# Attention whose probabilities below the diagonal are turned by DMA, in an order timed for all engines

## The chip, the cores and the metric

The program runs on one core of one Trainium2 chip. The metric is the device time in microseconds (us) of one execution. Three runs of the kernel before took 3117.63, 3124.31 and 3127.85 us; the median is 3124.31. One more execution was profiled, and the views below are of that one. The engines are named as the profile names them: PE is TensorE (PEld its weight loads), DVE is VectorE, ACT is ScalarE, POOL is GpSimd, SP is SyncE, which issues DMAs.

## What is computed

The program is a trunk of two layers on 2048 rows of 1024 numbers: a Mamba-2 mixer, then latent attention with 16 heads, an output projection and a norm. The change is in the attention alone. Its heart in the reference:

```python
def causal_block_attention(q_nope, q_rope, k_nope, k_rope, v):
    ...
        s = jnp.einsum('bqhd,bkhd->bhqk', q_nope[:, q0:kv_len], k_nope[:, :kv_len]) + \
            jnp.einsum('bqhr,bkr->bhqk', q_rope[:, q0:kv_len], k_rope[:, :kv_len])
        s = s.astype(jnp.float32) * scale
        mask = (q0 + local)[:, None] >= jnp.arange(kv_len)[None, :]
        p = jax.nn.softmax(jnp.where(mask, s, -jnp.inf), axis=-1).astype(v.dtype)
        outs.append(jnp.einsum('bhqk,bkhd->bqhd', p, v[:, :kv_len]))
```

## The kernel before

Attention (`heads`, from L1214) works in jobs: head h of 16 by block qb of four blocks of 512 queries. A job has four row groups j of 128 queries. Each looks at the keys up to its own diagonal, cut into chunks of up to 512 (`cuts`). All operands are pairs of f16 numbers, a high and a low half, so that products come close to f32.

For a row group and chunk, TensorE makes the scores with three products (`mm3`, L86 to L88) in a PSUM bank, and adds the mask at the diagonal (L1257). VectorE takes the row maximum from PSUM (L1258), and over the chunks of a row group a small reduction (L1262). ScalarE takes the exponential (L1269) into a buffer `Pr` in SBUF, f32, and its sum.

The products with V need the probabilities the other way round, keys on the rows. So `turn` (L1277) makes, for 128 keys, up to four 128x128 f32 transposes on TensorE into a PSUM bank (L1282). ScalarE evicts the high half to f16 (L124), VectorE the low half (L125), into a buffer `PTs`. `values` (L1288) adds the two products with V (L1292, L1293). A finished job is evicted (L1299) and stored by two DMAs, one from SP (L1301), one accumulating from POOL (L1305). K, V and Q of the next head are loaded by DMAs from POOL (L1184, L1185, L1190, L1196 to L1198).

What sets the order: on TensorE the program's own order, in which the table CREDIT says after each score chunk how many turns (T) and products with V (V) follow, 20 chunks behind (LAG):

```python
        for credit in ahead():
            step += 1
            if step > LAG:
                for what in credit:
                    work(what)
```

The other engines' order is left to a scheduler that goes by priority. After attention `back` (L1350) loads its output again and multiplies it with the output weights, which ACT (L1368) and POOL (L1369) split.

Of the kernel before, what the change touches and what calls it, by code (L numbers as in the profile page):

```python
# [11 lines left out]
BF16 = mybir.dt.bfloat16  # L12
# [24 lines left out]
NP = 24  # L37
# [29 lines left out]
C1, C2, C3 = 6.28125, 1.93500518798828125e-3, 3.01991598196e-7  # L67


class Net:  # L70
# [374 lines left out]
    def constants(self, cp):  # L445
# [6 lines left out]
        self.mk = cp.tile([P, 2 * P], BF16, name="mk")  # L452
# [5 lines left out]
    def layer_constants(self, cp):  # L458
# [13 lines left out]
        nc.vector.memset(self.mk[:, P:], NEG)  # L472
# [24 lines left out]
        nc.vector.tensor_copy(self.mk[:, 0:P], self.mask)  # L497
# [681 lines left out]
    def load_k(self, h, lo, hi):  # L1179

        nc, ts = self.nc, slice(lo * TB, hi * TB)
        if lo == 0:
            self.keys[h] = self.t(self.hp, "K", [96, 2, T], F16, bufs=2)
        nc.gpsimd.dma_start(self.keys[h][0:64, :, ts], self.kn_d[h * 64:(h + 1) * 64, :, ts])  # L1184
        nc.gpsimd.dma_start(self.keys[h][64:96, :, ts], self.kr_d[:, :, ts])  # L1185

    def load_v(self, h):

        V = self.vals[h] = self.t(self.xq, "xT", [P, T // P, P], F16, bufs=8)
        self.nc.gpsimd.dma_start(V, self.v_d[:, h * P:(h + 1) * P].rearrange("(k p) d -> p k d", p=P))  # L1190

    def load_q(self, h, n):

        nc, ts = self.nc, slice(n * TB, (n + 1) * TB)
        Q = self.quer[h, n] = self.t(self.xq, "xT", [96, 2, TB], F16, bufs=8)
        nc.gpsimd.dma_start(Q[0:64], self.qn_d[h * 64:(h + 1) * 64, :, ts])  # L1196
        nc.gpsimd.dma_start(Q[64:80], self.q1_d[h * 16:(h + 1) * 16, :, ts])
        nc.gpsimd.dma_start(Q[80:96], self.q2_d[h * 16:(h + 1) * 16, :, ts])  # L1198
# [7 lines left out]
    def attention(self):  # L1206
        with ExitStack() as ctx:
# [3 lines left out]
            with self.tc.manual_schedule(engines={mybir.EngineType.PE}):  # L1211
                self.heads(sp)

    def heads(self, sp):  # L1214
        nc, v = self.nc, self.nc.vector
        begun = []
        keys, vals, quer = self.keys, self.vals, self.quer

        def cuts(kv):

            out, at = [], 0
            while at < kv:
# [323 lines left out]
```

## Time and profile before

| | us |
|---|---|
| median of three runs | 3124.31 |
| the profiled execution | 3126.91 |
| its span | 3125.1 |
| attention: first score product to last eviction | 2059.6 to 2938 |
| PE busy over the span | 3033.6 (97%) |
| DVE busy over the span | 2297.6 (74%) |
| ACT busy over the span | 1963.6 (63%) |
| POOL busy over the span | 609.5 (20%) |

In the views, a group's row reads: line, engine, operation, out<-in with partitions x elements, count, then busy us and mean ns of one, then the idle time ahead of it and what ended that. A duration is that of one record; records of one engine overlap a little, since an instruction begins while the one before drains. The window rows give busy time per engine in a stretch, with the count of instructions in brackets, the granted TensorE clock, the DMA share and GB/s. The chain of waits follows the work that ended last.

### The profile page before, as it was taken

The numbers are of one execution on the slowest core, as the hardware profiler recorded it, in microseconds if no ns is written. First come the engines' busy times: TensorE is split into PE (matmuls) and PEld (weight loads), VectorE is DVE, ScalarE is ACT, GpSimd is POOL, SyncE is SP. The second block draws the span as 40 slices with busy tenths as digits, with TensorE's granted clock in tenths as the row PEclk, the third lists the DMA queues.
The fourth block names the chain that finished last, engine by engine and source line by source line (L and its number), as shares of the span: only waits on it lengthen the run. The fifth ranks groups of instructions, "written<-read, shape, count | busy, mean of one in ns | idle before, by whom it ended". The sixth has DMA issues, their size and how long they took to land.

```text
span 3125.1 us, 50616 instructions
## 1 busy us (share of the span) xinstructions
PE 3033.6 (97%) x17815; PEld 1946.3 (62%) x17815; DVE 2297.6 (74%) x4548; ACT 1963.6 (63%) x4952; POOL 609.5 (20%) x855
## 2 busy tenths in 40 slices
PE   8999999999999999999999999999999999999998
PEld 6777754556556665556665455456666666666687
DVE  6878887788776687776755644468888888888676
ACT  7888576665656465654643433368888888888522
POOL 1222022111221112211111212222222222222100
PEclk9999999999999999999999999999999999999999
DMA  5343667655465454754457556632232323233485
GB/s 179 120 135 107 214 201 256 192 157 179 150 220 179 129 161 128 239 192 129 143 159 270 173 163 202 190 96 55 58 64 55 68 53 66 56 73 89 110 270 163
DMA packets 217138, 456.78 MB, mean 146 GB/s; under 512 B 29154, under 2 KB 71138, under 8 KB 215444
## 3 DMA queue, kind: packets, MB, share of 16 engines
q1 hardware_dynamic: 188980, 375.54, 38.2%
q0 software_dynamic: 27904, 78.02, 9.6%
q8 instruction: 140, 2.29, 0.3%
q14 instruction: 114, 0.93, 0.1%
HBM read 332.21 MB, written 121.25 MB: 145 GB/s over the span
## 4 chain that ended last, share of the span: by engine, by line
PE 52%; issue 10%; DVE 9%; ACT 8%; DMA 5%; POOL 3%; SPq 1%; POOLq 0%; ACTq 0%; DVEq 0%
PE mm L86 10%; PE mm L87 10%; PE mm L88 10%; PE tr L1282 7%; PE tr L1292 3%; PE tr L1293 3%; DVE cacc L691 2%; PE tr L86 1%; PE tr L88 1%; PE tr L87 1%; DMA wraw<-in_ssm_w_in_dram 1%; DMA big<-cumT 1%; PE tr L895 1%; ACT Pr L1269 1%; ACT Xw L888 1%
## 5 line engine op out<-in xcount | busy, mean ns | idle before, releaser
L125 DVE SCALAR_TENSOR_TENSOR PTs<-tr,PTs 128x512 f16<-128x512 f32 (+3 forms) x640 | 373.1, 605 | 96.2 <-ACT PTs L124 90.2
L1269 ACT ACTIVATE Pr<-mm,nm 128x512 f32<-128x512 f32 (+2 forms) x631 | 398.7, 642 | 15.0 <-DVE nm L1262 14.2
L124 ACT ACTIVATE PTs<-tr 128x512 f16<-128x512 f32 (+3 forms) x640 | 331.0, 545 | 115.8 <-PE tr L1282 106.8
L1258 DVE TENSOR_REDUCE mx<-mm 128x1 f32<-128x512 f32 (+2 forms) x569 | 336.1, 615 | 21.0 <-PE mm L88 17.7
L1282 PE MATMUL tr<-pack,Pr 128*128 128x128 f32 x2176 | 318.0, 273 | 2.2 <-ACT Os L1299 2.0
L86 PE MATMUL mm<-xT,wsp 128*128 128x512 f16 (+1 forms) x800 | 308.7, 386 | 0.3 <-ACT wsp L116 0.3
L87 PE MATMUL mm<-xT,wsp 128*128 128x512 f16 (+1 forms) x800 | 306.2, 383 | 0.0
L88 PE MATMUL mm<-xT,wsp 128*128 128x512 f16 (+1 forms) x800 | 304.9, 383 | 0.5 <-DVE wsp L117 0.5
L1282 PEld LDWEIGHTS tr<-pack,Pr 128*128 128x128 f32 x2176 | 253.6, 141 | 69.7 <-ACT Os L1299 2.8
L86 PE MATMUL mm<-wsp,xT 128*128 128x512 f16 (+2 forms) x640 | 233.9, 367 | 6.3 <-ACT craw L685 5.1
L691 DVE SCALAR_TENSOR_TENSOR cacc<-craw,pack,cacc 128x512 f32<-128x512 f32 x288 | 217.1, 773 | 28.4 <-ACT cacc L689 26.6
L87 PE MATMUL mm<-wsp,xT 128*128 128x512 f16 (+2 forms) x640 | 233.4, 365 | 1.4 <-DVE wsp L125 1.3
L88 PE MATMUL mm<-wsp,xT 128*128 128x512 f16 (+2 forms) x640 | 233.0, 365 | 0.0
L86 PE MATMUL mm<-K,xT 96*128 96x512 f16 (+2 forms) x639 | 224.0, 350 | 8.2 <-ACT Pr L1269 6.7
L88 PE MATMUL mm<-K,xT 96*128 96x512 f16 (+2 forms) x639 | 223.0, 349 | 0.0
L87 PE MATMUL mm<-K,xT 96*128 96x512 f16 (+2 forms) x639 | 222.4, 348 | 0.0
L1292 PE MATMUL tr<-PTs,xT 128*128 128x512 f16 (+3 forms) x640 | 221.4, 347 | 0.1
L1293 PE MATMUL tr<-PTs,xT 128*128 128x512 f16 (+3 forms) x640 | 219.5, 347 | 0.0
L86 PE MATMUL mm<-wsp,yT 128*128 128x512 f32 x512 | 210.4, 412 | 1.9 <-DVE sz L721 1.3
L87 PEld LDWEIGHTS <-xT 128*128 128x128 f16 (+1 forms) x1280 | 125.5, 98 | 130.8 <-issue 34.8
L844 POOL TENSOR_TENSOR Xp<-Xw,Xp 128x512 fp32r<-128x512 f32 x64 | 86.6, 1353 | 609.1 <-ACT Xp L843 579.2
L87 PE MATMUL mm<-wsp,yT 128*128 128x512 f32 x512 | 204.2, 399 | 0.0
(457 smaller groups left out, 6965.1 us busy)
## 6 DMA issues: line engine op xcount, KB each, us to landing
wsp<-wo_d SPq DMA_DIRECT2D x96, 512.0 KB, 4.0
wsp<-w_d SPq DMA_DIRECT2D x68, 512.0 KB, 4.4
wraw<-in_ssm_w_in_dram SPq DMA_DIRECT2D x128, 256.0 KB, 3.1
big<-cumT SPq DMA_DIRECT2D x64, 512.0 KB, 4.9
wo_d<-wsp SPq DMA_DIRECT2D x32, 512.0 KB, 3.4
w_d<-wsp SPq DMA_DIRECT2D x32, 512.0 KB, 3.4
st<-w_d SPq DMA_DIRECT2D x56, 256.0 KB, 3.0
wsp<-wu_d SPq DMA_DIRECT2D x28, 512.0 KB, 3.8
```

The costliest lines, as they stand in the source:

```text
L86: mm(out, l_hi, r_hi, start=start, stop=False)
L87: mm(out, l_hi, r_lo, start=False, stop=False)
L88: mm(out, l_lo, r_hi, start=False, stop=stop)
L124: self.nc.scalar.activation(hi, src, AF.Copy, scale=scale)
L125: self.nc.vector.scalar_tensor_tensor(lo, src, scale, hi, ALU.mult, ALU.subtract)
L691: nc.vector.scalar_tensor_tensor(acc, raw[:, k:k + TB], wk[k], acc, ALU.mult, ALU.add)
L844: nc.gpsimd.tensor_tensor(u[:, 1], x, u[:, 0].bitcast(F32), ALU.subtract)
L1258: v.tensor_reduce(mx[:, n:n + 1], s[:, :w], AX.X, ALU.max, negate=nb == 1)
L1269: nc.scalar.activation(x[:, :w], s[:, :w], AF.Exp, bias=nm, accum_out=sums[h][:, at, n:n + 1])
L1282: nc.tensor.transpose(pt[:, j * P:(j + 1) * P], st["P"][j][kb], self.ident)
L1292: nc.tensor.matmul(st["O"][:, c], vals[h][:, kb, :], u[:, 0], start=kb == 0, stop=False)
L1293: nc.tensor.matmul(st["O"][:, c], vals[h][:, kb, :], u[:, 1], start=False, stop=kb == nk - 1)
```

## The change

Attention's order is now written out for all five engines before anything is issued. A class `Pace` plays the jobs through with a fixed duration for each step and a number of buffers, and records the order in which the steps begin; `heads` then issues them in that order, and the scheduler leaves all engines as they are. The steps: S scores, M maximum, N shift, E exponential; T turn on TensorE, A and B the evictions of its high and low half; V products with V; F, O eviction and store; R, Y, Z the row sums.

Of the six chunks of 512 keys below the diagonal that a head has (one in block 1, two in block 2, three in block 3), five take another way (TURNED): H copies the 128x512 f32 of `Pr` to f16 on VectorE, L subtracts it from `Pr` on GpSimd for the low half, both in one buffer `HL`, and X is one DMA from SP that transposes the 128x1024 of both halves into a tile `PX`. Four such DMAs (one per row group) fill a `PX`, from which V reads directly. The four diagonal chunks and one more stay on TensorE. There are six `HL`, three `PX` and 18 `Pr` buffers (24 before).

Besides: the diagonal chunks have their exact width of 128 to 512 (before, 256 at least); the factor 2^15 moves from the evictions into the exponential's shift (PSHIFT), which makes N one or two small operations on each of 256 row groups; a score may be in any of eight PSUM banks; the loads of K, V and Q are issued from SP in place of POOL.

```diff
-NP = 24
-LAG = 20
-DEPTH = 2
-CREDIT = (
-    (("VT",), ("TV",), ("VT",), ("TV",)),
-    (("", "VTVT"), ("", "TTVV"), ("", "TTVV"), ("", "TTVV")),
-    (("TT", "", "VVTV"), ("TV", "", "VTTV"), ("TV", "", "TTVV"), ("TTV", "", "TVV")),
-    (("T", "", "", "VVTTVTV"), ("T", "V", "", "VTTVTV"), ("T", "V", "V", "TVTTV"), ("TV", "V", "", "TVTVT")),
-)
+ENGINES = ("PE", "ACT", "DVE", "POOL", "SP")
+BUFS = dict(ps=8, Pr=18, PTs=5, HL=6, PX=3)
+SCORED = 5
+DMA_DELAY = 4000
+TURNED = ((), (0,), (0, 1), (0, 1))
+def DVE(n):
+    return 62 + n * 1.042, 135
+PSHIFT = 10.397207708399179
...
+class Pace:
...
+    def __init__(self, turned):
+        self.turned, self.now, self.count = turned, 0.0, 0
+        self.jobs = [(h, qb) for h in range(NH) for qb in range(NB)]
...
+    def run(self):
+        while True:
+            for e, waiting in self.ready.items():
+                if self.until[e] <= self.now:
+                    fit = sorted((w for w in waiting if w[2]()), key=lambda w: w[:2])
+                    if fit:
+                        waiting.remove(fit[0])
+                        fit[0][3]()
+            if self.until["PE"] <= self.now:
+                self.tensor()
+            if not self.coming:
+                break
+            self.now = self.coming[0][0]
+            while self.coming and self.coming[0][0] <= self.now:
+                heapq.heappop(self.coming)[2]()
+        assert not (self.todo_s or self.todo_t or self.todo_v)
+        return self.order
...
+    def tensor(self):
+        f = self.free
+        if self.sums and f["ps"] > 0:
+            return self.rows(self.sums.pop())
+        if self.todo_s and f["ps"] > 0 and self.scored < SCORED:
+            return self.scores(*self.todo_s.pop())
+        if self.todo_t and f["ps"] > 0 and f["PTs"] > 0:
+            n, k = self.todo_t[-1]
+            if all((n, j, k // 4) in self.probs for j in range(self.first(n, k), 4)):
+                return self.turn(*self.todo_t.pop())
+        if self.todo_v and self.todo_v[-1] in self.pairs:
+            if self.todo_v[-1][0] in self.opened or f["ps"] > 0:
+                return self.values(*self.todo_v.pop())
...
+    def high(self, n, j, c):
+        self.give(HL=-1, PX=-((n, c) not in self.dma))
+        self.dma.setdefault((n, c), 4)
+        def low():
+            self.issue("POOL", ("L", n, j, c), 1364, 60, moved)
+        def moved():
+            self.give(Pr=1)
+            self.queue("SP", 1, lambda: self.issue("SP", ("X", n, j, c), 1300, DMA_DELAY, landed))
+        def landed():
+            self.give(HL=1)
+            self.dma[n, c] -= 1
+            if not self.dma[n, c]:
+                for k in range(4 * c, 4 * c + 4):
+                    self.pairs[n, k] = "PX"
+        self.issue("DVE", ("H", n, j, c), 345, 130, lambda: self.queue("POOL", 1, low))
...
-            with self.tc.manual_schedule(engines={mybir.EngineType.PE}):
+            with self.tc.manual_schedule():
...
+    def load_q(self, h, n, q=None):
+        q, ts = q or self.nc.gpsimd, slice(n * TB, (n + 1) * TB)
         Q = self.quer[h, n] = self.t(self.xq, "xT", [96, 2, TB], F16, bufs=8)
-        nc.gpsimd.dma_start(Q[0:64], self.qn_d[h * 64:(h + 1) * 64, :, ts])
-        nc.gpsimd.dma_start(Q[64:80], self.q1_d[h * 16:(h + 1) * 16, :, ts])
...
-                def exp(n, at=4 * qb + j, parts=parts, banks=banks, nm=nm, p=p):
-                    s, w = banks[n]
-                    x = self.t(sp, "Pr", [P, TB], bufs=NP)
-                    nc.scalar.activation(x[:, :w], s[:, :w], AF.Exp, bias=nm, accum_out=sums[h][:, at, n:n + 1])
-                    for c in range(0, w, P):
-                        p[(parts[n][0] + c) // P] = x[:, c:c + P]
...
-        def turn(h, qb, kb, st):
-            jj = max(kb - 4 * qb, 0)
-            pt = self.t(self.pp, "tr", [P, TB], bufs=4)
-            for j in range(jj, 4):
-                nc.tensor.transpose(pt[:, j * P:(j + 1) * P], st["P"][j][kb], self.ident)
-            c = slice(jj * P, TB)
-            u = self.t(sp, "PTs", [P, 2, TB], F16, bufs=5)
-            self.pair16(u[:, 0, c], u[:, 1, c], pt[:, c], PSCALE)
-            return u[:, :, c], c
...
+        def S(n, j, c):
+            h, qb = jobs[n]
+            if j == c == 0:
                 if qb == 0:
                     sums[h] = self.t(sp, "sum", [P, 16, 4], bufs=3)
                     nc.gpsimd.memset(sums[h], 0.0)
...
+                if h + 1 < NH:
+                    if qb == 2:
+                        self.load_k(h + 1, 0, NB, nc.sync)
+                        self.load_v(h + 1, nc.sync)
+                    self.load_q(h + 1, qb, nc.sync)
+            Q, K, w = quer[h, qb], keys[h], pace.width(n, j, c)
+            s, tag = bank("mm")
+            qs, ks = slice(j * P, (j + 1) * P), slice(c * TB, c * TB + w)
+            self.mm3(s[:, :w], Q[:, 0, qs], Q[:, 1, qs], K[:, 0, ks], K[:, 1, ks], True, c < qb)
+            if c == qb:
+                nc.tensor.matmul(s[:, w - P:w], self.idb, self.mk, start=False, stop=True)
+            if c == 0:
+                shifts[n, j] = self.t(sp, "nm", [P, 1], bufs=4)
+                maxima[n, j] = self.t(sp, "mx", [P, 4], bufs=4)
+            banks[n, j, c] = s, tag, w
+        def M(n, j, c):
+            s, _, w = banks[n, j, c]
+            v.tensor_reduce(maxima[n, j][:, c:c + 1], s[:, :w], AX.X, ALU.max, negate=True)
+        def N(n, j):
+            qb, m, nm = jobs[n][1], maxima.pop((n, j)), shifts[n, j]
+            if qb == 1:
+                v.tensor_scalar(nm, m[:, 0:1], m[:, 1:2], PSHIFT, ALU.min, ALU.add)
+                return
+            if qb:
+                v.tensor_reduce(nm, m[:, :qb + 1], AX.X, ALU.min)
+            v.tensor_scalar(nm, nm if qb else m[:, 0:1], PSHIFT, None, ALU.add)
+        def E(n, j, c):
+            h, qb = jobs[n]
+            s, tag, w = banks.pop((n, j, c))
+            x = probs[n, j, c] = self.t(sp, "Pr", [P, TB], bufs=BUFS["Pr"])
+            nc.scalar.activation(x[:, :w], s[:, :w], AF.Exp, bias=shifts[n, j],
+                                 accum_out=sums[h][:, 4 * qb + j, c:c + 1])
+            used[tag] -= 1
+        def H(n, j, c):
+            u = halves[n, j, c] = self.t(sp, "HL", [P, 2, TB], F16, bufs=BUFS["HL"])
+            v.tensor_copy(u[:, 0], probs[n, j, c])
+        def L(n, j, c):
+            u = halves[n, j, c]
+            nc.gpsimd.tensor_tensor(u[:, 1], probs.pop((n, j, c)), u[:, 0], ALU.subtract)
+        def X(n, j, c):
+            if (n, c) not in moved:
+                moved[n, c] = self.t(sp, "PX", [P, 8, TB], F16, bufs=BUFS["PX"])
+            u = halves.pop((n, j, c)).rearrange("p s c -> p (s c)")
+            nc.sync.dma_start(moved[n, c][:, :, j * P:(j + 1) * P], u, transpose=True)
+        def T(n, k):
+            jj = pace.first(n, k)
+            pt, tag = bank("tr")
+            for j in range(jj, 4):
+                nc.tensor.transpose(pt[:, j * P:(j + 1) * P],
+                                    probs[n, j, k // 4][:, k % 4 * P:(k % 4 + 1) * P], self.ident)
+            turned[n, k] = pt, tag, slice(jj * P, TB)
+        def A(n, k):
+            pt, tag, c = turned[n, k]
+            u = self.t(sp, "PTs", [P, 2, TB], F16, bufs=BUFS["PTs"])
+            nc.scalar.activation(u[:, 0, c], pt[:, c], AF.Copy)
+            turned[n, k] = pt, tag, c, u
+        def B(n, k):
+            pt, tag, c, u = turned[n, k]
+            v.tensor_tensor(u[:, 1, c], pt[:, c], u[:, 0, c], ALU.subtract)
+            turned[n, k] = u[:, 0, c], u[:, 1, c]
+            used[tag] -= 1
+        def V(n, k):
+            h, qb = jobs[n]
+            if n not in outs:
+                outs[n] = *bank("tr"), 4 * qb + 4
+            o, tag, left = outs[n]
+            if (n, k) in turned:
+                hi, lo = turned.pop((n, k))
+            else:
+                hi, lo = (moved[n, k // 4][:, s * 4 + k % 4] for s in range(2))
+            c = slice(pace.first(n, k) * P, TB)
+            nc.tensor.matmul(o[:, c], vals[h][:, k, :], hi, start=left == 4 * qb + 4, stop=False)
+            nc.tensor.matmul(o[:, c], vals[h][:, k, :], lo, start=False, stop=left == 1)
+            outs[n] = o, tag, left - 1
...
+        def O(n):
+            h, qb = jobs[n]
+            o = outs.pop(n)
+            od = self.o_d[h * 64:(h + 1) * 64, qb * TB:(qb + 1) * TB]
+            nc.sync.dma_start(od, o[0:64, :])
+            nc.gpsimd.dma_start(od, o[64:128, :], accum_op=ALU.add)
+            if h == NH - 3:
+                self.load_wo(qb)
+        steps = dict(S=S, M=M, N=N, E=E, H=H, L=L, X=X, T=T, A=A, B=B, V=V, F=F, O=O, R=R, Y=Y, Z=Z)
+        for what, *where in pace.run():
+            steps[what](*where)
```

How the instructions move. On TensorE, in the third head, before: four turns (`pack` holds the identity) stand between the products with V for one block of keys and the next.

```order
L1282 MATMUL tr_23273<-pack,Pr_22957 128x128
L1282 MATMUL tr_23273<-pack,Pr_23023 128x128
L1282 MATMUL tr_23273<-pack,Pr_23100 128x128
L1282 MATMUL tr_23273<-pack,Pr_23170 128x128
L1292 LDWEIGHTS xT_21890
L1292 MATMUL tr_23076<-PTs_23230,xT_21890 128x128
```

At such a place now, again TensorE in the third head: after the last diagonal block, the products read a `PX` with no turn ahead of them.

```order
L1508 MATMUL tr_23289<-PTs_23382,xT_21859 128x128
L1507 LDWEIGHTS xT_21859
L1507 MATMUL tr_23289<-PX_23079,xT_21859 128x512
L1508 LDWEIGHTS xT_21859
L1508 MATMUL tr_23289<-PX_23079,xT_21859 128x512
```

Moved: 16 turns per such chunk are gone from TensorE's order, and V now waits for a DMA there. On VectorE before, in the third head: maxima (`mx`), shifts (`nm`) and evictions (`PTs`) alternate.

```order
L1258 TENSOR_REDUCE mx_22956<-mm_22989 128x1
L1262 TENSOR_REDUCE nm_22955<-mx_22956 128x1
L125 SCALAR_TENSOR_TENSOR PTs_23000<-tr_22997,PTs_23000 128x256
L125 SCALAR_TENSOR_TENSOR PTs_23005<-tr_23003,PTs_23005 128x128
L125 SCALAR_TENSOR_TENSOR PTs_23015<-tr_23010,PTs_23015 128x512
```

VectorE now, in the fourth head (CAST is step H, L1493 step B):

```order
L1465 CAST HL_23308<-Pr_23179 128x512
L1465 CAST HL_23316<-Pr_23230 128x512
L1444 TENSOR_REDUCE mx_23302<-mm_23297 128x1
L1465 CAST HL_23329<-Pr_23252 128x512
L1444 TENSOR_REDUCE mx_23302<-mm_23323 128x1
L1493 TENSOR_TENSOR PTs_23327<-tr_23312,PTs_23327 128x384
L1444 TENSOR_REDUCE mx_23302<-mm_23333 128x1
L1465 CAST HL_23361<-Pr_23287 128x512
L1493 TENSOR_TENSOR PTs_23356<-tr_23341,PTs_23356 128x256
L1452 TENSOR_REDUCE nm_23301<-mx_23302 128x1
L1453 TENSOR_SCALAR nm_23301<-nm_23301 128x1
```

Moved: the evictions of the five chunks are gone; the casts stand in ones and twos between maxima, and 124 of the later 319 directly behind another cast. POOL before only issues DMAs and clears the sums (`xT` is a Q or V tile); its order now, for the casts just shown, is that of their subtractions.

```order
L1190 DMA xT_21890<-v_d 128x16x128
L1324 MEMSET sum_23178 128x64
L1305 DMA o_d<-Os_21755 64x512
L1196 DMA xT_21892<-qn_d 64x2x512
L1197 DMA xT_21892<-q_d 16x2x512
```

```order
L1540 DMA o_d<-Os_23293 64x512
L1469 TENSOR_TENSOR HL_23308<-Pr_23179,HL_23308 128x512
L1469 TENSOR_TENSOR HL_23316<-Pr_23230,HL_23316 128x512
L1469 TENSOR_TENSOR HL_23329<-Pr_23252,HL_23329 128x512
L1469 TENSOR_TENSOR HL_23361<-Pr_23287,HL_23361 128x512
```

Moved: the loads went to SP, where they stand between the transposing DMAs, and a subtraction follows each cast on POOL.

More of the change, by code (lines that the diff above doesn't have):

```diff
@@ L1317, in heads, with bank @@
-        jobs = [(h, qb) for h in range(NH) for qb in range(NB)]
-        states = [{"P": []} for _ in jobs]
-        sums = {}
-        def ahead():
-            for n, (h, qb) in enumerate(jobs):
+        pace = Pace(TURNED)
+        jobs = pace.jobs
+        used = {"mm": 0, "tr": 0}
+        sums, shifts, maxima, banks, probs, turned, halves, moved, outs = ({} for _ in range(9))
+        def bank(first):
+            tag = first if used[first] < 4 else "tr" if first == "mm" else "mm"
+            used[tag] += 1
+            return self.t(self.pp, tag, [P, TB], bufs=4), tag
```

244 lines of the change are left out of this document (139 added, 105 removed).

## The prediction

> **What bounds the kernel now.** I read the busy times by window first, because the edit touches one stage only. Attention runs from the first turned chunk at 2074 us to the last eviction at 2938 us:
>
> ```profile
> core 0: us, PE busy (x) PEld busy (x) DVE busy (x) ACT busy (x) POOL busy (x), PEclk, DMA share, GB/s
> 2074.00:2938.00 864.00, 854.76 (x5584) 563.68 (x5582) 734.38 (x1500) 716.60 (x1975) 196.48 (x294) 1.00 0.28 61
> 2938.00:2950.00 12.00, 9.62 (x42) 7.33 (x41) 2.14 (x3) 1.11 (x3) 0.82 (x1) 0.98 0.80 197
> ```
>
> TensorE is busy for 854.8 of 864 us at full granted clock, so in this stage it is the bound and it loses only 9 us. VectorE (734, 85%) and ScalarE (717, 83%) have about 15% of room, and GpSimd (196) stands almost idle. Busy time of TensorE is not the same as work at its peak, so I then read the groups of this window and the chain of waits:
>
> ```profile
> L125 DVE SCALAR_TENSOR_TENSOR PTs<-tr,PTs 128x512 f16<-128x512 f32 (+3 forms) x640 | 373.1, 605 | 96.2 <-ACT PTs L124 90.2
> L1282 PE MATMUL tr<-pack,Pr 128*128 128x128 f32 x2175 | 317.8, 273 | 2.2 <-ACT Os L1299 2.0
> ```
>
> ```profile
> 2930.75 0.44 PE tr L1282 x4
> 2937.74 0.60 ACT Os L1299
> 2949.07 0.50 PE mm L86
> ```
>
> The record of one turn (273 ns) overlaps its neighbours. In the chain four turns take 0.44 us, so one costs the path 0.109 us, and 2176 of them cost 237 us of the 864. Almost nothing waits in front of them (2.2 us). VectorE idles for ScalarE's PTs (90 us), so it is a follower now.
>
> **What is taken off TensorE.** Per head, ten chunks of probabilities exist: four diagonal, six below. Five of the six leave TensorE: 5 x 16 = 80 turns per head, 1280 of 2176. That is 1280 x 0.109 = 139.5 us. The first row block of each head is now 128 wide, not 256: three products and a mask of 128 fewer columns, 4 x 0.053 us x 16 heads = 3.4 us (a quarter of the 512-column step of 0.216 us between 2911.69 and 2911.91 below). The products with V stay the same in number and width. TensorE's own need becomes 854.8 - 139.5 - 3.4 = 712 us.
>
> ```profile
> 2911.69 0.38 PE L1292 MATMUL tr<-PTs,xT 128*128 128x512 f16 x1
> 2911.91 0.38 PE L1293 MATMUL tr<-PTs,xT 128*128 128x512 f16 x1
> ```
>
> **What it does to ScalarE and VectorE.** A chunk that is turned by DMA needs no PSUM evictions. 80 pairs of 128x512 become 20 per head; 320 of each of these two evictions go:
>
> ```profile
> 2300.82 1.28 DVE L125 SCALAR_TENSOR_TENSOR PTs<-tr,PTs 128x512 f16<-128x512 f32 x2
> 2301.80 0.61 ACT L124 ACTIVATE PTs<-tr 128x512 f16<-128x512 f32 x1
> 2302.28 0.71 ACT L1269 ACTIVATE Pr<-mm,nm 128x512 f32<-128x512 f32 x1
> ```
>
> Two on VectorE take 1.28 us with one tail of about 0.08, so 0.60 each; on ScalarE the next instruction starts 0.48 after the eviction. ScalarE falls to 717 - 320 x 0.48 = 563 us and cannot bind. VectorE loses 320 x 0.60 = 192 us and gains 320 casts of 128x512 f32 to f16 in SBUF (step H). No such cast is in the trace; the nearest is a one-source SBUF operation of the same size, and the nearest in GpSimd's new work is its f32 add/subtract:
>
> ```profile
> L1001 DVE TENSOR_SCALAR yt<-sz x4: 427/428/617, 1587.6 to 1863.8; 128x512 f32<-128x512 f32 x4
> L1262 DVE TENSOR_REDUCE nm<-mx x192: 135/156/158, 2064.2 to 2918.3; 128x1 f32<-128x2 f32 x64, 128x1 f32<-128x3 f32 x64, 128x1 f32<-128x4 f32 x64
> L844 POOL TENSOR_TENSOR Xp<-Xw,Xp x64: 1255/1288/2115, 89.7 to 1571.7; 128x512 fp32r<-128x512 f32 x64
> ```
>
> I take 0.428 less the same tail, 0.345 us: 320 x 0.345 = 110 us (ends: 0.345, or 0.60 if it runs like the eviction, +82 us). The shifts change from 192 small reductions to 128 reductions and 256 one-column operations, 192 more at 0.16 = 31 us. VectorE's own need: 734 - 192 + 110 + 31 = 683 us, below TensorE's 712. Without anything else the stage would be TensorE's.
>
> **The price that decides: VectorE and GpSimd share something.** GpSimd gains 320 subtractions (step L) of 1.29 us, 413 us, and gives up issuing the loads of K, V and Q. Here is what its operations do to VectorE's in the Mamba stage:
>
> ```profile
> 239.21 1.65 POOL L844 TENSOR_TENSOR Xp<-Xw,Xp 128x512 fp32r<-128x512 f32 x1
> 239.62 1.79 DVE L902 TENSOR_TENSOR y<-y,yt 128x512 f32<-128x512 f32 x1
> ```
>
> ```profile
> L902 DVE TENSOR_TENSOR y<-y,yt x60: 678/692/1796, 105.2 to 1573.3; 128x512 f32<-128x512 f32 x60
> L896 DVE TENSOR_TENSOR y<-y,tr x64: 670/686/690, 87.3 to 1571.6; 128x512 f32<-128x512 f32 x64
> L211 DVE TENSOR_SCALAR rr<-ri x4: 156/654/1216, 351.1 to 1414.2; 1x2 int32<-1x2 int32 x4
> ```
>
> L902 has both operands in SBUF. Alone it takes 0.69; started 0.41 us into GpSimd's Xp it took 1.79, and it ended 0.55 after that did, as if it could begin only when GpSimd was about done. L896 has one operand in PSUM and never exceeds 0.690. A one-source SBUF operation (L211, L1001) shows the same jump, 0.156 to 1.216 and 0.427 to 0.617. So maxima and evictions, which read PSUM, are safe beside L, and H is not: it reads and writes SBUF with one source. H runs beside L by design, since each L starts when its H ends and the next H follows soon.
>
> The Trainium skill, SBUF — State Buffer, section Who interferes with whom, states just this: a copy in a two-port mode and a GpSimd operation exclude one another for a whole instruction, while an operation with one SBUF input outside these modes doesn't contend. The rows above agree; it speaks against this change.
>
> The size: with a stage of about 800 us, L runs for 413/800 = 52% of it. An H that comes at any moment then waits 0.52 x 1.29/2 = 0.33 us; 320 of them, 107 us. Ends: 0 (each H slips in just before its L) and 320 x 1.29 = 413. I take 107, because the order has both kinds: 124 of the 319 later H stand directly behind another H and can start before the first one's L, the others have reductions and evictions between and meet a running L. The 256 one-column operations could wait in the same way, 256 x 0.33 = 86 us; I take 0, since one element per row gives a second port nothing to do where L211 has two, and keep 86 in the range.
>
> Behind a waiting H, VectorE's queue holds maxima and evictions: the next exponentials wait for the maxima, PSUM banks come free late, and TensorE starves. So these microseconds land on the path as soon as VectorE's sum passes TensorE's: 683 + 107 = 790 against 712. GpSimd itself stands at 196 less its 210 issues plus L:
>
> ```profile
> L1196 POOL DMA_DIRECT2D xT<-qn_d x56 | 34.5, 617 | 247.5 <-PE tr L1312 180.4 <-PE mm L1257 66.9
> L1198 POOL DMA_DIRECT2D xT<-q_d x56 | 32.2, 575 | 0.0
> L1197 POOL DMA_DIRECT2D xT<-q_d x56 | 29.2, 521 | 0.0
> L1190 POOL DMA_DIRECT2D xT<-v_d x14 | 17.0, 1212 | 55.0 <-PE mm L1257 55.0
> L1184 POOL DMA_DIRECT2D K<-kn_d x14 | 7.5, 537 | 0.0
> L1185 POOL DMA_DIRECT2D K<-kr_d x14 | 7.1, 507 | 0.0
> ```
>
> 196 - 127 + 413 = 482 us, and it waits for H in turn; at most 110 more. It does not bind.
>
> **The transposing DMAs (step X).** 320 of 128 x 1024 f16, 256 KB each, all from SP's queue, 84 MB in all. The trace has no transposing DMA. The nearest rows are a plain load of the same size, a load in 256-byte pieces, and what it costs a queue to issue one:
>
> ```profile
> st<-w_d SPq DMA_DIRECT2D x56, 256.0 KB, 3.0
> xT<-v_d POOLq DMA_DIRECT2D x16, 512.0 KB, 6.1
> L1301 SPq DMA_DIRECT2D o_d<-Os x64: 445/446/514, 2082.4 to 2938.4; - x64
> ```
>
> Issue: between 0.45 (one piece per row) and 1.21 (L1190, sixteen); at 1.2, 384 us, with 289 other issues at 0.45 it is 514 us of SP, hidden. Landing: 3 us if transposing costs nothing extra, 6 us if small pieces cost twice. Six H/L buffers hold a chunk for about 0.4 + 1.3 + 1.2 + 6 = 9 us, so six in 9 us, 1.5 us per chunk and 480 us in all: hidden in 804. I take 0. At what rate it stops being hidden is rival D. The Trainium skill, DMA: Bandwidth & Descriptors, section Latency and other measured facts, gives 261 GB/s for a transposing DMA with a strided middle dimension, by which one would take an estimated 1.0 us and all 322 us; that would be hidden too, and no run here shows it yet. The moved loads on SP stand behind X's that wait for GpSimd; they are issued about a head early, 804/16 = 50 us, which covers them.
>
> **Sum.** VectorE 790, plus the 9 us that the bounding engine lost before, plus about 5 at the end: the last chunk now goes L 1.3, X and landing 3 to 4 before its products. 804 against 864, 60 us less. The eviction-to-output gap of 11 us after 2938 (quoted in the chain) stays. The profiled execution took 3126.9 us (span 3125.1 and 1.8 around it): 3067. The median of the runs is 2.6 lower than that execution, so 3065.
>
> **Rivals.**
> - B, TensorE stays the bound. H mostly finds GpSimd between two L, which needs waits below (712 - 683)/320 = 0.09 us each. 712 + 9 + 5 = 726, 138 us less: 2987. For it: 124 H stand directly behind another one, and VectorE has slack before it binds (683 against 712). Against: L fills half the stage, so most other H must meet one.
> - C, the wait eats it all, slower. The place is VectorE at H. The waits reach 864 - 14 - 683 = 167 us when an H waits 0.52 us instead of 0.33; from there on the kernel is slower. If each of the 195 H that don't stand directly behind another one waits a whole L: 195 x 1.29 = 252, stage 949, 85 us more: 3210. For it: L902's 1.79, a nearly whole wait, and each L starts just behind its H; the order was made with engines that don't hinder each other. Against: then all engines wait, and gaps grow.
> - D, the transposing DMAs become the bound: one at a time at 2.66 us or more per chunk (850/320). At the 3.0 us of the plain load with no overlap, 960 + 14, 110 more: 3237. For it: nothing here shows two of them in flight. Against: the DMA share is 0.28 in this stage. The Trainium skill, VectorE: DVE Perf Modes, section The three transpose paths, lists 1309 ns for one 128x128 block by DMA; eight to a chunk one after another would be 10 us by estimate, far beyond that point.
> - E, VectorE lands about where TensorE was (790 with about 60 of the small operations' 86): within 9 us of before.
>
> **Numbers.** Forecast 0.48, B 0.20, C 0.14, D 0.10, E 0.08. Below 0.3% (9 us) this measurement can't tell from no change. Faster: B and nearly all of the forecast, 0.66; same: E and the forecast's upper edge, 0.10; slower: C and D, 0.24. The forecast's own range is 3000 to 3120 (waits of 0.12 to 0.5 us per H). The full range is 2982, just under B, to 3180, which takes in the nearer half of C; beyond lie the rest of C and D, a little under 0.2.
>
> **What the next profile would show.** TensorE's busy share of the stage should fall to about 88%, with idle before the score products put down to ScalarE's Pr or to VectorE; 896 turns. The cast should have a minimum near 0.43 us and a median well above it, up to 1.7; L should be 1.3 with a tail to 1.7. Casts that are all at 0.43 with TensorE at 98% make it B; casts with a median over 0.9 make it C. If VectorE's idle is put down to a DMA (H waiting for its buffer) or TensorE's to PX, the transposes are late, and it is D. Should the small shift operations show 1 us, the 86 us that I left out are there.

## The result and the profile after

The changed kernel takes 3227.29 us (median of 4 runs, 3222.88 to 3231.51) against 3124.76 (3117.63 to 3127.85) of the kernel before on the same chip: ratio 1.0331, 95% interval 1.0308 to 1.0355. It is slower by 103 us; forecast were 3065 us, and the range ended at 3180. The profiled execution has a span of 3221.1 us.

First the stage by windows, with the columns of the prediction's first fence. Attention now runs from 2074 to 3035 us:

```profile
2074.00:3035.00 961.00, 775.96 (x4292) 436.78 (x4290) 772.43 (x1676) 572.04 (x1651) 438.67 (x401) 0.92 0.77 141
```

961 us in place of 864; 804 were forecast. No engine is full: TensorE is busy for 81% of the stage, VectorE for 80%, ScalarE for 60%, GpSimd for 46%. The work came out much as worked out (VectorE 772 against 790, ScalarE 572 against 563, GpSimd 439 against 482). What was not foreseen is idle time everywhere, and the eighth column: the granted clock of TensorE, 1.00 before, is 0.92 as a mean over the stage. The stage is 157 us over the forecast: 64 of it are TensorE's busy time (776 against 712), and 93 its idle time (961 - 776 = 185, against 804 - 712 = 92). In the trace's record of the clock, 22 spells at half clock last 150 us in all, and TensorE is busy for 112 of these. Half of that, 56 of the 64 us, is lost to the slow clock; the other 8 are work over the forecast (720 us at full clock).

Next the new operations: durations in ns as minimum/median/maximum, and for the DMA the median us from issue to landing:

```profile
L1465 DVE CAST HL<-Pr x320: 406/417/10078, 2061.1 to 3022.8; 128x512 f16<-128x512 f32 x160
L1469 POOL TENSOR_TENSOR HL<-Pr,HL x320: 1147/1394/1679, 2061.6 to 3026.6; 128x512 f16<-128x512 f32 x160
L1475 SPq DMA_TRANSPOSE PX<-HL x320: 1231/1277/2567, 2062.8 to 3028.5; - x160
L1453 DVE TENSOR_SCALAR nm<-nm x128: 141/154/155, 2068.3 to 3000.4; 128x1 f32<-128x1 f32 x128
...
PX<-HL SPq DMA_TRANSPOSE x320, 3.2
```

The waits of the stage (us in total, times, longest) then show where the engines stood:

```profile
PE mm L279 <- ACT Pr L1459: 147.9, 109, 6.9
POOL HL L1469 <- DVE HL L1465: 142.8, 66, 14.0
POOL o_d L1540 <- DMA o_d<-Os: 139.6, 26, 8.9
POOL o_d L1540 <- ACT PTs L1488: 120.5, 27, 9.1
...
ACT Pr L1459 <- POOL HL L1469: 110.2, 73, 7.1
ACT Pr L1459 <- DVE nm L1453: 107.2, 62, 6.3
...
POOL o_d L1540 <- ACT Pr L1459: 42.2, 7, 8.3
```

L1540 is step O on GpSimd, the accumulating store of a finished job, which adds the upper 64 rows to what SP's plain store (L1539) has put into the same rows of `o_d`, and so waits until that has landed. GpSimd stood in front of it for over 300 us (the three rows give 302). Two of the rows name ScalarE, but the timeline speaks for the landing there too: whatever the row names, GpSimd starts the store between 2.8 and 4.7 us after SP issued the plain store. TensorE waited 148 us for exponentials. These waited 110 us for the subtraction L1469, which is what gives a buffer Pr back, and 107 us for the shift `nm` on VectorE. One such stall in the timeline (start, length, engine; in brackets the idle time before, and what ended it):

```profile
2507.10 5.77 SPq L1475 DMA_TRANSPOSE PX<-HL  x2
2509.93 0.60 ACT L1515 ACTIVATE Os<-tr 128x512 f32<-128x512 f32 x1 [0.75 <-PE tr L1508]
2512.93 0.58 SPq L1389 DMA_DIRECT2D xT<-qn_d  x1
2514.89 0.54 SPq L1539 DMA_DIRECT2D o_d<-Os  x1
2518.18 0.83 POOL L1540 DMA_DIRECT2D o_d<-Os  x1 [6.18 <-DMA o_d<-Os]
2518.78 4.72 POOL L1469 TENSOR_TENSOR HL<-Pr,HL 128x512 f16<-128x512 f32 x4
2520.22 0.58 ACT L1459 ACTIVATE Pr<-mm,nm 128x384 f32<-128x384 f32 x1 [6.06 <-POOL HL L1469]
2520.94 0.58 PE L279 MATMUL mm<-K,xT 96*128 96x512 f16 x1 [5.80 <-ACT Pr L1459]
```

The output tile is ready at 2510.5. SP is still at two transposing DMAs, then at three loads of Q, and issues the plain store at 2514.89. Its landing lets GpSimd go on at 2518.18, 3.3 us later. Four subtractions are queued behind the accumulating store; the first frees a Pr at 2520.2, the exponential behind it frees a PSUM bank, and TensorE starts again after 5.8 us. That recurs about once a head: 20 gaps of more than 2 us hold 102 of TensorE's idle us, and 16 of them lie for more than half of their length in GpSimd's stand at L1540 or the 2 us after it (both from the timeline). Such places cover 436 of the 961 us, so that this alone proves little; e1 below is the test.

The clock, from windows of 1 us of TensorE alone (busy time, clock, DMA share, GB/s) over the same stall:

```profile
2514.00:2515.00 1.00, 1.00 (x10) 1.00 0.48 135
...
2517.00:2518.00 1.00, 0.00 (x0) 1.00 0.01 2
2518.00:2519.00 1.00, 0.00 (x0) 0.71 0.00 0
2519.00:2520.00 1.00, 0.00 (x0) 0.50 0.50 47
...
2524.00:2525.00 1.00, 1.00 (x5) 0.50 0.41 94
2525.00:2526.00 1.00, 1.00 (x5) 0.88 1.09 205
2526.00:2527.00 1.00, 1.00 (x8) 1.00 0.38 80
```

After some 3.3 us without work the clock falls to one half, and it stays there for four us after the work is back at 2520.94 (the microsecond from 2524 holds 5 matmuls, the one from 2514 10). A stall is paid a second time: each of the 16 gaps over 3 us in this stage is followed by such a spell, or has one begin in it.

The kernel before had the same wait, and paid nothing for it:

```profile
POOL o_d L1305 <- ACT PTs L124: 139.3, 17, 11.4
POOL o_d L1305 <- ACT Pr L1269: 117.2, 32, 11.1
...
POOL o_d L1305 <- DMA o_d<-Os: 86.9, 14, 22.8
```

There only loads for the next head were queued behind it.

### The profile page after: what moved, and what is told of

Read it like the earlier page. It is cut to its first block, busy times and chain, and to the rows that moved or that the text cites. A ratio compares the mean times of both kernels' runs of the same rounds, so it can differ in the third digit from the quotient of the medians.

```text
span 3221.1 us, 49216 instructions
## 1 busy us (share of the span) xinstructions
PE 2956.2 (92%) x16535; PEld 1820.5 (57%) x16535; DVE 2340.8 (73%) x4739; ACT 1820.9 (57%) x4632; POOL 849.7 (26%) x950
## 5 line engine op out<-in xcount | busy, mean ns | idle before, releaser
L1459 ACT ACTIVATE Pr<-mm,nm 128x512 f32<-128x512 f32 (+3 forms) x544 | 342.1, 637 | 233.3 <-POOL HL L1469 110.2
L1469 POOL TENSOR_TENSOR HL<-Pr,HL 128x512 f16<-128x512 f32 x320 | 384.0, 1319 | 213.7 <-DVE HL L1465 149.0
L1444 DVE TENSOR_REDUCE mx<-mm 128x1 f32<-128x512 f32 (+3 forms) x544 | 330.3, 615 | 134.1 <-PE mm L281 116.3
L279 PE MATMUL mm<-K,xT 96*128 96x512 f16 (+4 forms) x552 | 204.2, 370 | 151.3 <-ACT Pr L1459 150.7
L280 PEld LDWEIGHTS <-xT 128*128 128x128 f16 (+1 forms) x1280 | 127.9, 100 | 278.3 <-issue 195.1
L1465 DVE CAST HL<-Pr 128x512 f16<-128x512 f32 x320 | 248.5, 801 | 3.2 <-ACT Pr L1459 1.8
L279 PE MATMUL mm<-wsp,yT 128*128 128x512 f32 x512 | 210.3, 411 | 3.5 <-DMA wsp<-wo_d 2.3
L1488 ACT ACTIVATE PTs<-tr 128x512 f16<-128x512 f32 (+2 forms) x318 | 145.0, 470 | 109.6 <-PE tr L1481 108.6
L280 PE MATMUL mm<-wsp,yT 128*128 128x512 f32 x512 | 204.6, 400 | 0.0
L281 PE MATMUL mm<-wsp,yT 128*128 128x512 f32 x512 | 203.7, 399 | 0.0
L280 PE MATMUL mm<-K,xT 96*128 96x512 f16 (+4 forms) x552 | 203.7, 369 | 0.0
L281 PE MATMUL mm<-K,xT 96*128 96x512 f16 (+4 forms) x552 | 202.8, 369 | 0.0
L281 PEld LDWEIGHTS <-xT 128*128 128x128 f16 (+1 forms) x1280 | 127.5, 100 | 124.4 <-issue 13.8
L279 PEld LDWEIGHTS <-xT 128*128 128x128 f16 (+1 forms) x1280 | 127.5, 100 | 112.0 <-issue 12.1
```

The costliest lines, as they stand in the source:

```text
L279: mm(out, l_hi, r_hi, start=start, stop=False)
L280: mm(out, l_hi, r_lo, start=False, stop=False)
L281: mm(out, l_lo, r_hi, start=False, stop=stop)
L1444: v.tensor_reduce(maxima[n, j][:, c:c + 1], s[:, :w], AX.X, ALU.max, negate=True)
L1459: nc.scalar.activation(x[:, :w], s[:, :w], AF.Exp, bias=shifts[n, j], accum_out=sums[h][:, 4 * qb + j, c:c + 1])
L1465: v.tensor_copy(u[:, 0], probs[n, j, c])
```

## The experiments

The theories. **Q**: GpSimd's queue; the subtractions stand behind the accumulating store. **L**: the casts on VectorE wait for GpSimd's running operation. **O**: the order itself is slower, whatever is turned by DMA. Each time below is the median of four or five runs beside the kernel before on the same chip; the ratio to it has a 95% interval. The runs were on several chips, and the kernel before took 3124.8 to 3129.4 us there, so differences of a few us between experiments are not to be read.

**e1_late_add** issues the accumulating store of a job only at the next job's O:

```
+        adds = []
...
-            nc.gpsimd.dma_start(od, o[64:128, :], accum_op=ALU.add)
...
+            while adds:
+                nc.gpsimd.dma_start(*adds.pop(0), accum_op=ALU.add)
+            adds.append((od, o[64:128, :]))
+            if n == len(jobs) - 1:
+                nc.gpsimd.dma_start(*adds.pop(0), accum_op=ALU.add)
```

> Only GpSimd's accumulating store of a finished job moves: it is issued behind the next job's store instead of with its own, so that the plain store it adds to has landed; 3227 us as changed. Theory Q (GpSimd's queue stands at this store for 321 us of the stage, the subtractions queue behind it, ScalarE waits for probability buffers and TensorE stands 5 us per head): waits at the store fall under 60 us, TensorE's long idle stretches go (some 90 us) and part of the lost clock comes back: 3085 to 3140. Theory L (the exclusion of cast and subtraction is what costs): at most 20 us less, 3205 or more. Theory O (a fixed order for all engines is the loss): at most 20 us less.

Measured: 3143.98 us, ratio 1.0057 (1.0036 to 1.0078), 83 us below the changed kernel. The stage by windows:

```profile
2074.00:2957.00 883.00, 766.49 (x4303) 429.84 (x4301) 770.50 (x1686) 567.99 (x1661) 448.83 (x404) 0.95 0.83 154
```

GpSimd's stand in front of this store falls from 312 us to 50 (its waits in the stage summed), with VectorE's busy time unchanged. Q holds, though the time is 4 us past its range, and it is most of the loss; the stage is still 79 us over the forecast.

**e2_cast_act** moves the cast (step H) to ScalarE, in the order and in the code:

```
-                self.queue("DVE", 3, lambda: self.high(n, j, c),
+                self.queue("ACT", 3, lambda: self.high(n, j, c),
...
-        self.issue("DVE", ("H", n, j, c), 345, 130, lambda: self.queue("POOL", 1, low))
+        self.issue("ACT", ("H", n, j, c), 494, 160, lambda: self.queue("POOL", 1, low))
...
-            v.tensor_copy(u[:, 0], probs[n, j, c])
+            nc.scalar.activation(u[:, 0], probs[n, j, c], AF.Copy)
```

> The cast H goes from VectorE to ScalarE, in the order's plan too; all else as changed. No VectorE instruction then waits for a subtraction (115 us of waiting in 320 casts) and VectorE sheds 250 us, ScalarE gains about 154 to some 725 us. Theory L: 100 us or more less, 3125 or under. Theory Q: the 5 us stalls at the accumulating store stay, 20 to 60 us less, 3165 to 3205. Theory O: within 30 us of 3227.

Measured: 3226.93 us, ratio 1.0322 (1.0305 to 1.0338).

```profile
2074.00:3038.00 964.00, 790.14 (x4336) 446.89 (x4335) 580.54 (x1379) 731.54 (x1989) 436.21 (x406) 0.91 0.78 142
```

VectorE lost 192 us of its busy time, the casts' waits among them, ScalarE gained 160, and the end did not move. L falls as the main cause, and Q's 20 to 60 us for this edit were missed as well. As long as GpSimd stands at the store, taking the cast's wait away gains nothing.

**e3_both** has both edits.

> Both of the foregoing. Theory Q: the late store does most, the cast on ScalarE adds a little as no engine but TensorE is then near full: 3040 to 3100. Theory L: as the cast alone, 3125 or under, with nothing from the store. Theory O: still over 3180.

Measured: 3082.81 us, ratio 0.986 (0.9843 to 0.9876).

```profile
2074.00:2894.00 820.00, 743.11 (x4287) 420.08 (x4285) 562.54 (x1363) 715.99 (x1969) 431.46 (x403) 0.96 0.92 166
```

With the store out of the way the same move is worth 61 us (3144.0 to 3082.8). Alone it was worth 0: the two waits hide one another, and only the order of removal decides how much each seems to cost.

**e4_order_only** leaves every chunk on TensorE, in the changed kernel's kind of order (`TURNED = ((), (), (), ())`).

> No chunk is turned by DMA (all ten on TensorE again); the order timed for all engines, the exact widths and the loads on SP stay. Theory O: slower than before by 60 us or more, 3185 and up. Theories Q and L: TensorE needs 851 of the stage's time again and GpSimd has no subtractions, so within 25 us of before: 3100 to 3150.

Measured: 3177.19 us, ratio 1.0165 (1.015 to 1.018).

```profile
2074.00:2988.00 914.00, 867.74 (x5570) 549.67 (x5569) 746.46 (x1684) 722.23 (x1975) 72.85 (x86) 1.00 0.30 58
```

```profile
POOL o_d L1540 <- DMA o_d<-Os: 413.0, 28, 29.4
POOL o_d L1540 <- ACT Pr L1459: 317.7, 25, 23.2
```

The time lies between the two ranges. Two things follow. GpSimd stands still longer at the store here, yet TensorE idles for only 46 us and keeps its full clock, since nothing but these stores is in that queue: the wait costs only through the subtractions behind it. And this list is 50 us longer than the stage before. That is a list for another mix of work, so it is no measure of what the order costs the changed kernel; e9 below, with the same rules, is much shorter. O stays open for ten chunks on TensorE.

**e5_load_no_lock** asks whether the 61 us were the wait or simply VectorE's work. It is e3_both with other work for VectorE:

```
             v.tensor_reduce(maxima[n, j][:, c:c + 1], s[:, :w], AX.X, ALU.max, negate=True)
+            if c in pace.turned[jobs[n][1]]:
+                v.tensor_reduce(self.t(sp, "junk", [P, 1], bufs=2), s[:, :335], AX.X, ALU.max)
```

> This is e3_both (late accumulating store, cast on ScalarE; 3082.8 us) with VectorE's load put back, but without the thing it shares with GpSimd: for each of the 320 chunks that go by DMA, VectorE reads 335 columns of the same PSUM bank a second time (an estimated 0.42 us each by the 605 ns of a 512-wide maximum at about 1.04 ns a column, 134 us in all; the cast took 0.417 where it didn't wait). VectorE's busy time in the stage would go from 562 to about 697 us. Theory L (what casts cost on VectorE is the wait for GpSimd): within 1% of e3_both, 3083 to 3110. Rival R (the 61 us between e1_late_add and e3_both are VectorE's plain load, not the wait): back to 3130 to 3150.

Measured: 3090.22 us, ratio 0.9863 (0.9842 to 0.9884).

```profile
2074.00:2900.00 826.00, 742.95 (x4321) 416.50 (x4320) 679.38 (x1694) 726.14 (x1987) 434.84 (x406) 0.98 0.93 166
```

117 us more of work that reads PSUM cost 7 us (by the ratios, 0.9863 against 0.986, nothing that can be told), and casts of about that size cost 61. So it is not VectorE's work as such. What is left is the wait, which e11 shows at work; but with the cast on another engine the order is timed anew as well, and these two were not taken apart.

**e8_cast_strided** is e1_late_add with a cast that steps by two elements, to take it out of its faster form:

```
-            v.tensor_copy(u[:, 0], probs[n, j, c])
+            v.tensor_copy(u[:, 0].rearrange("p (c t) -> p t c", t=2),
+                          probs[n, j, c].rearrange("p (c t) -> p t c", t=2))
```

> e1_late_add (3144.0 us) with the cast left on VectorE but read and written with a step of two elements, so that it runs as the one-source f32 operation without the faster mode (0.417 us for 512 columns is quicker than the 605 of a 512-wide reduction). Theory L, in the form that the wait for GpSimd belongs to the faster mode: all casts at about 0.6 us with no tail to 10 us; VectorE's busy time 770 - 123 + 320 x 0.19 = 708 us, and 3085 to 3120. Rival R (VectorE's load alone, or any SBUF-to-SBUF operation waits): the casts keep a mean far over their median, or the added 60 us of work count in full: 3144 to 3200.

Measured: 3145.87 us, ratio 1.0044 (1.0027 to 1.0061).

```profile
L1466 DVE CAST HL<-Pr x320: 431/453/4119, 2068.2 to 2947.4; 128x512 f16<-128x512 f32 x160
```

The casts wait as before, against L's form. They also run nearly as fast as before (453 ns), so the step of two probably left them in the form that was to be excluded. The run decides nothing about which form of a cast waits.

**e7_load_later** is e3_both with the next head's first two loads of Q moved to the middle of the second block:

```
-                    self.load_q(h + 1, qb, nc.sync)
+                    if qb > 1:
+                        self.load_q(h + 1, qb, nc.sync)
+            if (j, c) == (2, 0) and qb == 1 and h + 1 < NH:
+                self.load_q(h + 1, 0, nc.sync)
+                self.load_q(h + 1, 1, nc.sync)
```

> e3_both with the next head's loads of Q for its first two row blocks issued in the middle of the second block instead of at the starts of the first and second. Theory S (SP's queue: in e3_both SP stood 77 us in front of the first load of Q, whose buffer is still being read by the products with V, and the transposing DMAs queued behind it came late, so TensorE waited 27 + 8 us for PX): these waits go, and with them part of the slow clock; stage 820 to about 785, 3040 to 3062. Rival (PX is late because GpSimd's subtraction is late behind casts on ScalarE, whoever is in SP's queue): the waits for PX stay, 3075 to 3090.

Measured: 3109.73 us, ratio 0.9935 (0.9917 to 0.9952), 27 us slower than e3_both. TensorE's wait for PX went from 26.9 to 34.0 us. But SP still stood 84 us in front of the loads of Q (all its rows at L1389), against 89 in e3_both: the edit hardly touched the stand that it was to remove. So the run decides nothing about theory S, and why it came out slower than both ranges wasn't pursued.

**e9_px4** is e3_both with other counts of buffers, `Pr=14` for 18 and `PX=4` for 3, in the same room.

> e3_both (3082.8 us) with four landing tiles PX instead of three and 14 buffers Pr instead of 18, so that both fill the same room; the order is timed anew with these counts. What is left in e3_both is TensorE's wait for PX (27 + 8 us, behind casts that wait 11 us and subtractions that wait 13 for a free tile) and for ScalarE's Pr (44). Theory P (the transposed chunks are late for want of landing room): the first of these goes, the second stays, 3045 to 3072. Rival T (the exponentials are held up by Pr buffers, of which there are fewer now): the wait for Pr grows by more than the 35 us, 3085 to 3120.

Measured: 3046.07 us, ratio 0.9741 (0.9725 to 0.9757), 78 to 81 us below the kernel before.

```profile
2074.00:2853.00 779.00, 724.16 (x4292) 412.73 (x4291) 557.12 (x1368) 717.30 (x1977) 433.92 (x404) 0.99 0.99 175
```

P holds, at the lower edge of its range: TensorE's idle time before the products with PX falls from 27 to 6 us, and the clock comes back to 0.99. This is the fastest version of the study.

**e10_no_add** is the changed kernel without line 1540 and with nothing else changed; it leaves out the addition of the upper 64 rows of each head's output.

> The changed kernel (3227.3 us) without GpSimd's accumulating store: the upper 64 rows of each head's output, which belong to the low half of V, are left out of the sum; all else, the casts on VectorE too, is as in the changed kernel. Theory Q (the subtractions stood behind the store that waits for SP's plain store to land): like e1_late_add, which still issues 64 of these stores at 0.85 us, or up to 20 us below it, 3120 to 3150. Rival L' (in the changed kernel the wait of casts is the loss and GpSimd's standing at the store only goes along with it): within 20 us of the changed kernel, 3207 to 3235.

Measured: 3106.06 us, ratio 0.9935 (0.9916 to 0.9955).

```profile
2074.00:2916.00 842.00, 740.07 (x4296) 417.87 (x4294) 749.56 (x1684) 566.10 (x1655) 398.67 (x340) 0.98 0.81 152
```

The whole store is worth 121 us, more than Q's range said: 83 are its wait, and about 38 are left for the store itself as e1_late_add still issues it, with the 50 us that GpSimd still stands there. Those 64 stores keep GpSimd for 64 x 0.83 = 53 us; VectorE's busy time is 21 us less without them. How the 38 divide wasn't tried.

**e11_px4_dve** is e9_px4 with the cast back on VectorE. With the store out of the way and room to land, it comes nearest to the case that the prediction's sum describes, though with 14 buffers `Pr` for 18. (e1_late_add, with the prediction's own counts, has a stage of 883 us.)

> e9_px4 (3046.1 us) with the cast back on VectorE, which is e1_late_add (3144.0) with four PX and 14 Pr. With the store out of the way and room to land, this is the case that the prediction's sum describes: VectorE as the bound. By that sum (683 us of work, the casts' waits, 9 us of idle, 5 at the end) the stage takes 790 to 810 us and the kernel 3050 to 3075. Rival K (VectorE's waits are not only its own time: GpSimd runs several subtractions in a row while one cast waits, maxima queue up behind, TensorE starves and slows): as e1_late_add, 3120 to 3150.

Measured: 3170.74 us, ratio 1.0125 (1.0097 to 1.0154); rival K, and beyond its range.

```profile
2074.00:2984.00 910.00, 787.18 (x4319) 442.65 (x4318) 788.01 (x1697) 577.93 (x1669) 450.23 (x404) 0.92 0.83 150
```

VectorE's 788 us are within 2 us of the prediction's 790, and the stage is 910, not 804. The timeline at a run of four casts, VectorE and GpSimd side by side:

```profile
2535.48 0.42 DVE L1466 CAST HL<-Pr 128x512 f16<-128x512 f32 x1
...
2535.98 1.16 POOL L1470 TENSOR_TENSOR HL<-Pr,HL 128x512 f16<-128x512 f32 x1 [5.68 <-DVE nm L1453]
2536.00 0.15 DVE L1454 TENSOR_SCALAR nm<-nm 128x1 f32<-128x1 f32 x1
2536.07 6.05 DVE L1466 CAST HL<-Pr 128x512 f16<-128x512 f32 x4
...
2537.50 1.27 POOL L1470 TENSOR_TENSOR HL<-Pr,HL 128x512 f16<-128x512 f32 x1 [0.36 <-DVE HL L1466]
...
2539.30 2.52 POOL L1470 TENSOR_TENSOR HL<-Pr,HL 128x512 f16<-128x512 f32 x2
```

Casts and subtractions take turns: the first cast, before any subtraction runs, takes 0.42. Of the next four, one slips in between (0.41), and three wait for the subtractions that their forerunners started: they take 1.34, 1.38 and 3.15 us, the last through two subtractions in a row. The four take 6.05 us together; three casts without a wait took 1.08 in the changed kernel, so four would take about 1.4. No maximum and no eviction gets through VectorE in that time. TensorE pays with a gap of 3.4 us in front of its turns, about one a head in this kernel (L1482, put down to VectorE's evictions), and with the clock (0.92).

## Why the prediction was wrong

Point by point, by its own steps.

- **TensorE's need, 712 us: right.** With the busy time at half clock counted half, the changed kernel has 720 us and e9_px4 716.
- **ScalarE 563, GpSimd 482, VectorE's work 683: right within 10%.** Measured are 572, 439, and 772 less the 123 us of the casts' waits, 649.
- **The casts' waits, 107 us: right as a sum; which casts wait depends on where GpSimd stands.** The 320 casts have a mean of 801 ns over a median of 417, 0.384 x 320 = 123 us. The prediction let 124 casts that stand directly behind another one go free (shifts between them not counted), "can start before the first one's L". In the changed kernel that is half true: these 124 waited 32 us in all, 0.26 each, and the other 196 waited 91, 0.46 each. Casts go free where GpSimd stands elsewhere (three in a row take 1.08 us at 2511.89, at the start of GpSimd's stand at the store). With the store out of the way it turns round: in e11_px4_dve the casts behind another cast waited 110 us and the others 14. Of the rows from which the prediction took the wait, one was no such case: the one L1001 of 0.617 us ran beside a DMA issue of GpSimd, not beside an operation. The Trainium skill, SBUF — State Buffer, section Who interferes with whom, says that, of a VectorE operation in a two-port mode and a GpSimd operation, whoever issues first holds the shared ports for a whole instruction. The runs agree that whole subtractions are waited for (which mode the cast runs in they don't show), and one cast took longer than one subtraction: 3.19 us, at 2503.05 in the changed kernel, while three subtractions ran for 3.63 us without a break.
- **"It does not bind", of GpSimd: the step that failed.** GpSimd was weighed by its work, 482 us of 800, and the wait at L1540 was not priced, though the trace before showed it (the three rows above). The subtractions were moved into a queue that already stood still for over 300 us a stage. This is a change that adds no wait and puts urgent work behind an old one. It costs 83 us (e1); with the store itself it is 121 (e10).
- **The sum as the largest engine's busy time plus 9 us of idle: failed as well.** The 9 us belonged to an engine that others feed and that had work queued up. Here VectorE stands in pieces of 1.3 to 6 us inside a ring (maximum, exponential, cast, subtraction, Pr) whose steps wait for one another. In e11 GpSimd's stand at the store is down to 11 us, VectorE has 788 us, and the stage takes 910. That the ring passes these pieces on is the reading of e11's timeline; no run changes it alone. The prediction's price for C, "then all engines wait, and gaps grow", is what happened, with the store's wait besides.
- **TensorE's clock: left out.** 56 of the 157 us over the forecast. The Trainium skill, TensorE: Matmul & The Clock Gate, section Part 1: The HAM clock gate, states that an idle window of about 3.4 us halves the clock and a busy one brings it back. The trace agrees in part: at 2518.4 the clock is halved after 3.3 us of idle time, and all spells at half clock in this stage last one, two or three times 3.41 us. But the idle time need not fill such a stretch: the spell that begins at 2866.58 follows one gap of 1.67 us.
- **The transposing DMAs, taken as hidden: right; rival D falls.** Issue takes 1.28 us (bounds 0.45 and 1.21 us, just exceeded), landing 3.2. TensorE waited 2.5 us for PX in the whole stage ("PE tr L1507 <- DMA PX<-HL"). The 1309 ns per block that the Trainium skill gives (VectorE: DVE Perf Modes, The three transpose paths) don't add up over the eight blocks of one DMA: its whole landing is 3.2 us. The transposes cost TensorE much more only in e3_both, once the rest ran faster (27 us).
- **The one-column operations' 86 us, taken as 0: right.** They take 139 to 215 ns and never wait.
- **Rival C** gave 3210 by the casts alone. That the time is near it is luck: e2_cast_act takes the casts' waits away and stays at 3227. **B** (TensorE stays the bound, 2987) and **E** are refuted by the time. TensorE's 712 us are not reached by e9_px4's 779 either: 12 us of busy time (8 of them slow clock) and 55 of idle time are left.

The 181 us between the changed kernel and e9_px4 go, in the order in which they were taken away, 83 to the store's wait, 61 to the casts' wait and 37 to the room for landing. Open remain: which form of a cast waits (e8), how the 38 us of the store itself divide, why e11 is 27 us slower than e1_late_add with its two counts changed, what holds the transposes up in e3 (e7), and what e4's list loses.

## What to carry to other kernels

Before work is moved to an engine that "stands almost idle", read what that engine stands in front of: a wait that is harmless while nothing is queued behind it becomes a stall of the whole ring once the ring runs through that queue. Then keep from the queue whatever waits for another engine's DMA, or issue it later, when it no longer waits (a few lines, 83 us). And price TensorE's stalls by their length. Over the stage of all twelve runs, 81 of 85 gaps over 3 us had a spell at half clock begin in them or within 3.4 us behind them, and 21 of 31 gaps of 2 to 3 us. Shorter ones count where they crowd (e1: clock 0.95, with five gaps over 2 us in its timeline), while 46 us in scattered pieces cost no clock (e4).

## What the hardware showed beyond that

- A cast from SBUF to SBUF on VectorE took 0.42 us alone and up to 10.1 us beside GpSimd (at 3002 us of the changed kernel, where GpSimd has two operations of 128x1024 on the output weights and then subtractions). A reduction that reads PSUM took no harm from the same neighbour: the 320 added ones of e5 took 490 to 501 ns each.
- The subtraction doesn't show the reverse. Its record has a median of 1.39 us in the changed kernel, but also in e2_cast_act, where VectorE casts nothing, and 1.16 in e1_late_add, where it does:

```profile
L1469 POOL TENSOR_TENSOR HL<-Pr,HL x320: 1148/1393/1509, 2074.7 to 3029.7; 128x512 f16<-128x512 f32 x160
L1470 POOL TENSOR_TENSOR HL<-Pr,HL x320: 1145/1165/1660, 2066.6 to 2947.5; 128x512 f16<-128x512 f32 x160
```

  The longer record belongs to subtractions queued directly behind one another, whose records overlap: the four at 2518.78 take 4.72 us together, 1.18 each.
- A transposing DMA of 256 KB from SBUF to SBUF holds SP's queue for 1.28 us and lands 3.2 us after its issue, about as fast as a plain load of that size (3.0).
